# A conformer block on one core: the output product by Strassen's scheme in half the tokens first, norm weights moved to the transposed side

## The chip, the cores and the metric

The kernel runs on 1 core of one Trainium2 chip. The metric is the device time of one execution in microseconds (us). Five engines work beside each other, each through its own queue in program order: PE (matrix products and transposes), DVE and ACT (tiles of 128 partitions, in SBUF or in PE's accumulators, the PSUM banks), POOL (tiles in SBUF) and SP, which issues the DMAs. PE's clock is granted at one of two levels; the profile prints the granted share (1.00 or 0.50, and mixtures in a stretch).

## The reference

T = 1024 tokens, D = 1024, an inner width of 2816. Only the end of the block matters here:

```
g_att, g_conv = split(sigmoid(gate_logits))
mix = (g_att * y_att + g_conv * (conv @ w_conv_out)) @ w_o
x   = layer_norm(ALPHA * x + mix, ln1_g, ln1_b)
u   = x @ w_up ;  a, b = split(u)
ffn = (gelu(causal_dwconv(a, 3 taps)) * b) @ w_down
x   = layer_norm(ALPHA * x + ffn, ln2_g, ln2_b)
```

`layer_norm` is (x - mean) * rsqrt(var + eps) * g + b over the 1024 columns. Results are fp32.

## The kernel before

Every fp32 operand is split in two parts, a rounded high part (ACT copy) and a low part (DVE subtraction); a product is three matmuls, hi·hi, lo·hi and hi·lo. One matmul takes 128 rows of a weight or input and 512 columns. The stages, by the profiled execution: projections, attention, convolution and gates up to about 550 us; the product with w_conv_out up to 594; the output product with `w_o`; the first norm; up (22 steps called quads, each a two by two Strassen product of 84 matmuls) from about 700 to 1147; down (seven Strassen products of 11 steps, 12 matmuls each) up to 1367; the last norm and the output.

The work around the change:

- **Output product (L825 to L851).** `mix` (L655 to L672) is kept in two token halves. Half 0 runs k by k into eight banks, 192 matmuls; then tiles 4 to 7 run one at a time, 48 matmuls each: 384 in all. `close_tile` (L683) takes the banks into `res[t]` with the residual and row sums, and its `norm` squares on ACT (L696) and applies mean, scale, weight and bias in two 128x1024 DVE operations (L705, L706).
- **`turn0` (L748) and `turn1` (L761).** They transpose the normed tiles by PE (32 transposes each; `res` of tiles 0 to 3, then 4 to 7) and form the parts `xfh`/`xfl` of the seven left operands of the up Strassen products. `turn0`, called after tile 5, makes products 1 and 2's, `turn1` those of 4, 5, 7, 6, 3, in four rounds over k; POOL makes 8 sums (L773, L774).
- **Up.** `quad` (L884) runs products 1, 3, 2, 5, 7, 6, 4 of one weight block; `prep_raw` and `prep_sums` (L802 to L815) prepare the next block's parts and its four POOL sums `wt`. The x1 tiles go to DRAM after the turns.
- **Down.** `next_step` keeps the loads, POOL's sums `dn` of weights (L958, 44 of them) and the parts `hl..` (two ACT copies, two DVE subtractions of 128x512, L972 to L975) a step or more ahead. `step_load` reloads a tile of x1 with every second load of products 5 and 6. After product 6 come `p1` additions, POOL's `p5` subtractions (L1093) and 16 joins into `resb` (L1088), 12 of them in one run; the closing of tiles uses `close_tile` again and one output DMA of 512 KB a tile.

Each engine's queue order is set by the scheduler from program order and priorities; what stands where is shown below.

Of the kernel before, what the change touches and what calls it, by code (L numbers as in the profile page):

```python
# [115 lines left out]
def build(ctx, tc, xT, x, w_v, w_in, w_ao, w_co, w_o, w_up, w_dn, par, rel, rows, out):  # L116
# [538 lines left out]
    mix = [[], []]  # L655
    for s in range(8):
        if s % 2 == 0:
            w = next_w()
        wys = tuple(v[:, (s % 2) * HT:(s % 2 + 1) * HT] for v in w)
        o = bank2()  # L660
        for h in range(2):
            strip(o[:, h, :], wys, cv, KA, h)
        V.tensor_mul(t2[s], o.rearrange("p h t -> p (h t)"), t2[s])
        V.tensor_add(t2[s], t2[s], t1[s])
        for h in range(2):
            hi, lo = sb(f"mxh{h}{s}", [P, HT], F32R), sb(f"mxl{h}{s}", [P, HT], F32R)
            m = t2[s][:, h * HT:(h + 1) * HT]
            S.activation(hi, m, AF.Copy)
            V.tensor_sub(lo, m, f32(hi))
            mix[h].append((hi, lo))  # L670
        sb.free(t1[s], t2[s])
# [6 lines left out]
    def close_tile(t, scale, g_bc, b_bc, out=None):  # L678


        r, st = res[t], st_r()
# [8 lines left out]

        def norm():
            V.tensor_add(m, st[:, 0:1], st[:, 1:2])
            V.tensor_scalar(z, m, -1.0 / D, None, op0=OP.mult)
# [11 lines left out]
            V.scalar_tensor_tensor(r, r, m, g_bc, op0=OP.subtract, op1=OP.mult)  # L705
            V.scalar_tensor_tensor(r, r, y, b_bc, op0=OP.mult, op1=OP.add)  # L706
            if out is not None:
                nc.sync.dma_start(out, r)

        return take, norm  # L710

    def close_tiles(ts, banks, *a, outs=None):
        norms = []
        for t in ts:
            take, norm = close_tile(t, *a, out=None if outs is None else outs[t])
            for c, o in enumerate(banks(t)):
                take(o, c)
            norms.append(norm)
        for norm in norms:
            norm()  # L720

    def single(t, i):

        if t % 2 == 0 or i == 2:
            return bank()
        return ps_v.tile([P, HT], F32, tag="pv", name="pv") if i else ps_t.tile([P, HT], F32, tag="tp", name="tp")

    g_bc, b_bc = sb("g1", [P, D]), sb("b1", [P, D])
    bcast(g_bc, 0)
    bcast(b_bc, 1)  # L730
# [3 lines left out]

# [11 lines left out]

    def turn0():

        for n in (1, 2):
            part(n)  # L750
            xs[n] = [sb(f"xs{n}{i}", [P, HT]) for i in range(4)]
        for k in range(KD):
            n, i = 1 + k // 4, k % 4
            tp = bank()
            turned(tp, 0, k)
            hi, lo = xf[n][i]
            S.activation(hi, tp, AF.Copy)
            V.tensor_sub(lo, tp, f32(hi))
            S.activation(xs[n][i], tp, AF.Copy)
# [423 lines left out]
```

## Time and profile before

| | us |
|---|---|
| median of 3 runs | 1381.43 (1380.97 to 1382.74) |
| the profiled execution, its own time | 1380.95 |
| its span | 1379.2 |
| PE busy | 1334.7 (97%) |
| DVE busy | 977.7 (71%) |
| ACT busy | 605.6 (44%) |
| POOL busy | 350.6 (25%) |

The span is what the trace covers; 1.75 us of the execution lie around it. A busy share says how long an engine had an instruction in work; PE's waits must be looked for in the stretches where its share falls.

### The profile page before, as it was taken

Reading aid. Unit: us, or ns where it says so; the run is one execution under the profiler, and the core shown is the slowest. Engines: PE = TensorE matmul, PEld = TensorE weight load, DVE = VectorE, ACT = ScalarE, POOL = GpSimd, SP = SyncE. Lnnn points to the kernel's source line nnn. Section 1 sums busy time; section 2 is a strip of 40 time slices with the busy share of each in tenths; the row PEclk is TensorE's granted clock in tenths of the full one; section 3 lists DMA queues with packets and bytes.
Section 4 is the critical chain, followed back from the end, with each engine's and each line's share of the span. In section 5 each row is a group of like instructions: output and inputs, shape, how many; then the busy total and the mean of one; then the engine's idle time right before and its main releaser. Section 6 shows DMA issues by size and latency. Waiting matters only on the chain.

```text
span 1379.2 us, 16028 instructions
## 1 busy us (share of the span) xinstructions
PE 1334.7 (97%) x6004; PEld 1082.0 (78%) x6004; DVE 977.7 (71%) x1399; ACT 605.6 (44%) x916; POOL 350.6 (25%) x247
## 2 busy tenths in 40 slices
PE   9999999999999999999959999999999999998996
PEld 8877887887888888888737888888888878777885
DVE  5278888887799935746596565566666558997668
ACT  4346555656661137322453433334333444443453
POOL 1000000000000000000055566565555546972000
PEclk9999999999999999999969999999999999999999
DMA  7011111112101111621123323332223247753323
GB/s 268 16 46 41 40 56 41 56 51 82 47 31 46 55 37 52 223 92 51 45 62 107 108 87 115 115 115 89 103 96 103 100 173 267 263 166 93 92 84 123
DMA packets 48495, 132.29 MB, mean 96 GB/s; under 512 B 5393, under 2 KB 5529, under 8 KB 45601
## 3 DMA queue, kind: packets, MB, share of 16 engines
q1 hardware_dynamic: 48416, 131.26, 27.8%
q8 instruction: 47, 0.77, 0.2%
q14 instruction: 32, 0.25, 0.1%
HBM read 101.07 MB, written 30.17 MB: 95 GB/s over the span
## 4 chain that ended last, share of the span: by engine, by line
PE 82%; DVE 9%; ACT 3%; POOL 3%; issue 2%; DMA 1%; POOLq 0%; DVEq 0%; SPq 0%; ACTq 0%
PE mm L196 6%; PE mm L197 6%; PE mm L198 6%; PE s L196 5%; PE s L197 5%; PE s L198 5%; PE s L821 4%; PE s L822 4%; PE s L823 4%; PE mm L822 2%; PE mm L823 2%; PE mm L821 2%; PE s L1051 2%; PE s L1052 2%; PE tp L456 2%; PE s L1050 2%
## 5 line engine op out<-in xcount | busy, mean ns | idle before, releaser
L196 PE MATMUL mm<-xh,whi 128*128 128x512 f32 x384 | 157.9, 411 | 2.0 <-ACT qq L266 2.0
L414 DVE SCALAR_TENSOR_TENSOR acc<-hpad,par,acc 128x1024 f32<-128x1024 f32 x120 | 152.3, 1278 | 0.7
L198 PE MATMUL mm<-xh,wlo 128*128 128x512 f32 x384 | 151.8, 395 | 0.0
L197 PE MATMUL mm<-xl,whi 128*128 128x512 f32 x384 | 151.5, 395 | 0.0
L809 POOL TENSOR_TENSOR wt<-quad 128x512 f32<-128x512 f32 x22 | 28.3, 1288 | 467.7 <-ACT junk L696 375.9
L180 ACT ACTIVATE whi<-wraw 128x1024 fp32r<-128x1024 f32 x40 | 42.4, 1060 | 109.3 <-PE s L197 65.8
L798 DVE TENSOR_TENSOR wrl<-quad,wrh 128x1536 fp32r<-128x1536 f32 x22 | 42.7, 1942 | 60.8 <-ACT wrh L797 60.8
L198 PEld LDWEIGHTS mm<-xh,wlo 128*128 128x128 f32 x384 | 72.2, 188 | 15.1
L958 POOL TENSOR_TENSOR dn<-dn,dn 128x512 f32<-128x512 f32 x44 | 73.7, 1697 | 32.7 <-DMA actr<-act_d 14.7
L196 PEld LDWEIGHTS mm<-xh,whi 128*128 128x128 f32 x384 | 72.4, 189 | 11.9 <-ACT qq L266 2.9
L197 PEld LDWEIGHTS mm<-xl,whi 128*128 128x128 f32 x384 | 72.7, 189 | 9.2
L821 PE MATMUL s<-xfh,w24h 128*128 128x512 f32 x176 | 73.5, 418 | 2.1 <-DVE uU L912 1.9
L822 PE MATMUL s<-xfh,w24l 128*128 128x512 f32 x176 | 68.8, 391 | 0.0
L823 PE MATMUL s<-xfl,w24h 128*128 128x512 f32 x176 | 68.8, 391 | 0.0
L458 ACT ACTIVATE pth<-tp 128x512 fp32r<-128x512 f32 (+3 forms) x96 | 41.5, 433 | 54.1 <-PE tp L456 53.5
L181 DVE TENSOR_TENSOR wlo<-wraw,whi 128x1024 fp32r<-128x1024 f32 x40 | 48.7, 1219 | 23.0 <-ACT whi L180 22.8
L459 DVE TENSOR_TENSOR ptl<-tp,pth 128x512 fp32r<-128x512 f32 (+3 forms) x96 | 46.8, 488 | 18.5 <-ACT pth L458 17.9
L1014 DVE SCALAR_TENSOR_TENSOR y<-a,par,y 128x1024 f32<-128x1024 f32 x22 | 38.6, 1756 | 29.3 <-ACT y L1013 29.3
L439 ACT ACTIVATE p<-p,st 128x640 f32<-128x640 f32 (+2 forms) x64 | 44.4, 694 | 28.6 <-DVE st L437 28.0
L821 PE MATMUL mm<-xfh,wrh 128*128 128x512 f32 x132 | 52.8, 400 | 3.1 <-ACT xfh L777 3.1
L1013 ACT ACTIVATE y<-a,par 128x1024 f32<-128x1024 f32 x22 | 27.4, 1245 | 62.4 <-POOL a L914 57.5
L812 POOL TENSOR_TENSOR wt<-wt,quad 128x512 f32<-128x512 f32 x22 | 54.1, 2458 | 0.9
(567 smaller groups left out, 3842.2 us busy)
## 6 DMA issues: line engine op xcount, KB each, us to landing
quad<-in_w_up SPq DMA_DIRECT2D x22, 1024.0 KB, 5.2
actr<-act_d SPq DMA_DIRECT2D x77, 256.0 KB, 2.7
wraw<-in_w_in SPq DMA_DIRECT2D x32, 512.0 KB, 3.5
act_d<-u SPq DMA_DIRECT2D x44, 256.0 KB, 2.0
dn<-in_w_dn SPq DMA_DIRECT2D x44, 256.0 KB, 4.0
act_d<-y SPq DMA_DIRECT2D x33, 256.0 KB, 2.3
res<-in_x SPq DMA_DIRECT2D x8, 512.0 KB, 5.8
wraw<-in_w_o SPq DMA_DIRECT2D x8, 512.0 KB, 3.5
```

Source lines behind the costliest of these rows:

```text
L181: V.tensor_sub(lo, raws[i], f32(hi))
L196: PE.matmul(o, ah, bh, start=first, stop=False)
L197: PE.matmul(o, ah, bl, start=False, stop=False)
L198: PE.matmul(o, al, bh, start=False, stop=last)
L414: V.scalar_tensor_tensor(a, hp[:, j:j + T], col(C_CW + c * TAPS + j), a, op0=OP.mult, op1=OP.add)
L439: S.activation(pt, pt, AF.Exp, bias=st[:, 0:1], scale=-1.0, accum_out=st[:, 1:2])
L459: last_lo[0] = V.tensor_sub(pl[:, :w], o[:, :w], f32(ph)[:, :w])
L812: G.tensor_add(t[:, 3], t[:, 2], b[:, 3])
L821: PE.matmul(o, wh, xh, start=go, stop=False, skip_group_check=not first)
L822: PE.matmul(o, wl, xh, start=False, stop=False, skip_group_check=not first)
L823: PE.matmul(o, wh, xl, start=False, stop=i == 3, skip_group_check=not first)
L958: G.tensor_add(dn[j][d], dn[j][d], dn[j][b])
```

## The change

- **Output product by Strassen's two by two scheme** over token halves and column halves: seven products of 48 matmuls (4 token tiles, 4 k blocks, 3 parts) in the order 1, 5, 6, 3, 2, 7, 4. `w_o` comes in four quadrants of 1 MB; POOL makes 16 sums of 128x512 for the weights (`wo_add`) and 16 more for the left forms (`m5`, `m7`); ACT and DVE make 14 pairs of 128x1024 parts of weights (`wo_parts`) and 28 pairs of 128x512 parts of left forms (16 pairs before). The rows of w_conv_out are relaid so that strips come in the order 0, 4, 1, 5, ...
- **Token half 0 is complete after product 2**, the fifth; its tiles are closed then. Statistics come from `bn_stats`/`bn_aggr` on DVE instead of the square on ACT; `plain` writes (x - mean) * rstd with one ACT operation, and the first norm's weight and bias are applied per partition where `turned` evicts the transposes.
- `turn0` comes before product 4, which completes half 1. **Products 1 and 2 of quads 0 and 1** (48 matmuls) run before `turn1`; `quad_first` and `begun` finish these two quads. `turn1` makes forms 4 and 7 in its rounds, then 5, 6 and 3 by 12 POOL sums in a chain.
- **x1 is stored without weight and bias.** Each of its 8 reloads is followed by one DVE `scalar_tensor_tensor` (times ALPHA and g1) and one POOL addition (b1), both 128x1024. The 16 joins of down become additions; 12 of them stand after `down(7)` in the program. Final tiles are closed in halves with two output DMAs of 256 KB each.

```diff
@@ output product
+    for i in range(4):
+        w = next_w()
+        for s, c in ((i, 0), (i + 4, 1)):
...
+        mix_form(1, i, a11)
+        G.tensor_sub(m5, a21, a22)
+        mix_form(5, i, m5)
+        G.tensor_sub(m5, m5, a11)
+        mix_form(6, i, m5)
+        G.tensor_add(m5, m5, a12)
+        mix_form(3, i, m5)
+        G.tensor_sub(m7[i], a11, a21)
...
+            V.scalar_tensor_tensor(rc, o, sign, rc, op0=OP.mult, op1=OP.add)
+            V.bn_stats(st[:, 6 * c:6 * c + 6], rc)
...
+        def plain():
+            m, y = norm()
+            V.scalar_tensor_tensor(z, m, -1.0, y, op0=OP.mult, op1=OP.mult)
+            S.activation(r, r, AF.Identity, bias=z, scale=y)
...
+    xb = banks_x()
+    wo_product(2, xb, 0)
+    wo_add(1, 3)
+    wo_parts(1, 0)
...
+    for t in range(4):
+        lns[t][0](0, xb[t])
+        lns[t][2]()
+    yb = banks_y()
+    wo_product(7, yb, 1)
...
+        S.activation(a, o, AF.Identity, bias=col(C_B1 + k), scale=col(C_G1 + k))
...
+    turn0()
     for t in range(4):
+        for i in range(4):
+            wo_mm(4, yb, 0, t, i, True)
+        lns[t + 4][0](0, yb[t])
+        lns[t + 4][2]()
...
+    for o, w, u in ((oa[0], wr, "1"), (oa[1], wr1, "1b")):
+        product(o, w, 0, 1, True)
+        S.activation(tmp[u], o, AF.Copy)
+        product(o, w, 2, 2, False)
     turn1()
@@ down
                 nc.sync.dma_start(res[t], x1_d[t])
+                V.scalar_tensor_tensor(res[t], res[t], ALPHA, g1_bc, op0=OP.mult, op1=OP.mult)
+                G.tensor_add(res[t], res[t], b1_bc)
...
+        V.tensor_add(r, r, o)
```

PE, where the transposes of half 0 stand. Before, they follow the last matmuls of tile 5 (`woh`, `mxh` are parts of w_o and of the mix), and 12 matmuls of tile 6 come after the first eight:

```order
L196 MATMUL pv_4876<-woh47_4662,mxh17_4458 128x512
L197 MATMUL pv_4876<-wol47_4663,mxh17_4458 128x512
L198 MATMUL pv_4876<-woh47_4662,mxl17_4459 128x512
L745 MATMUL mm_4940<-ident_68,res0_4466 128x128 [waits DMAHW1_49,DVE_49]
L745 MATMUL mm_4940<-ident_68,res1_4467 128x128 [waits DMAHW3_49,DVE_49]
L745 MATMUL mm_4940<-ident_68,res2_4468 128x128 [waits DMAHW5_49]
L745 MATMUL mm_4940<-ident_68,res3_4469 128x128 [waits DMAHW6_49]
L745 MATMUL mm_4948<-ident_68,res0_4466 128x128
L745 MATMUL mm_4948<-ident_68,res1_4467 128x128
L745 MATMUL mm_4948<-ident_68,res2_4468 128x128
```

After, they follow the last matmuls of product 7 (`wop1`, `mfh7`), and the first of product 4 (`mfh4`) come behind:

```order
L732 MATMUL s2_4945<-wop1l_4495,mfh73_4804 128x512
L733 MATMUL s2_4945<-wop1h_4494,mfl73_4805 128x512
L845 MATMUL mm_5020<-ident_68,res0_4496 128x128 [waits DMAHW5_49,Activation_49]
L845 MATMUL mm_5020<-ident_68,res1_4497 128x128 [waits DMAHW1_49,Activation_49]
L845 MATMUL mm_5020<-ident_68,res2_4498 128x128 [waits DMAHW2_49,Activation_49]
L845 MATMUL mm_5020<-ident_68,res3_4499 128x128 [waits DMAHW3_49,Activation_49]
L845 MATMUL mm_5031<-ident_68,res0_4496 128x128
L845 MATMUL mm_5031<-ident_68,res1_4497 128x128
L845 MATMUL mm_5031<-ident_68,res2_4498 128x128
L845 MATMUL mm_5031<-ident_68,res3_4499 128x128
L731 MATMUL s2_4944<-wop0h_4173,mfh40_4876 128x512 [waits DVE_49]
```

The transposes stand behind all of products 1, 5, 6, 3, 2 and 7, and in front of all of product 4; all four tiles are needed for the first eight.

PE at the end of `turn1`'s forms. Before, the form of product 7 (`xfh7`) follows that of 3 (`xfh3`), the one that needs the longest chain of sums, and product 2 (`xfh2`, parts made long ago) stands between:

```order
L821 MATMUL s2_5421<-xfh70_5177,w13h_5149 128x512 [waits DVE_49,PE_49]
L822 MATMUL s2_5421<-xfh70_5177,w13l_5150 128x512
L823 MATMUL s2_5421<-xfl70_5178,w13h_5149 128x512
L821 MATMUL s2_5421<-xfh71_5179,w13h_5149 128x512
L822 MATMUL s2_5421<-xfh71_5179,w13l_5150 128x512
L823 MATMUL s2_5421<-xfl71_5180,w13h_5149 128x512
L821 MATMUL s2_5421<-xfh72_5181,w13h_5149 128x512 [waits Activation_49]
L821 MATMUL mm_5420<-xfh32_5197,wrh_4846 128x512 [waits Activation_49]
L822 MATMUL mm_5420<-xfh32_5197,wrl_4847 128x512
L822 MATMUL s2_5421<-xfh72_5181,w13l_5150 128x512
L823 MATMUL s2_5421<-xfl72_5182,w13h_5149 128x512 [waits DVE_49]
L823 MATMUL mm_5420<-xfl32_5198,wrh_4846 128x512 [waits DVE_49]
```

After, product 3 of quad 1 (`wr1`, into bank `pv`) stands ahead of product 7 of quad 0:

```order
L921 MATMUL mm_5522<-xfl53_5393,w13h_5211 128x512 [waits DVE_49]
L919 MATMUL pv_5608<-xfh30_5417,wr1h_5206 128x512 [waits Activation_49]
L920 MATMUL pv_5608<-xfh30_5417,wr1l_5207 128x512
L921 MATMUL pv_5608<-xfl30_5418,wr1h_5206 128x512 [waits DVE_49]
L919 MATMUL pv_5608<-xfh31_5421,wr1h_5206 128x512 [waits Activation_49]
L920 MATMUL pv_5608<-xfh31_5421,wr1l_5207 128x512
L921 MATMUL pv_5608<-xfl31_5422,wr1h_5206 128x512 [waits DVE_49]
L919 MATMUL pv_5608<-xfh32_5425,wr1h_5206 128x512 [waits Activation_49]
L920 MATMUL pv_5608<-xfh32_5425,wr1l_5207 128x512
L919 MATMUL s2_5523<-xfh70_5296,w13h_5211 128x512 [waits Activation_49]
L920 MATMUL s2_5523<-xfh70_5296,w13l_5212 128x512
```

Products 7, 6 and 3 of quad 0, 36 matmuls, now stand behind a matmul that needs the form `xfh32`, the third of the last four that are made.

POOL at the end of up and the start of down (`dn` weight sums of down, `u22`, `u5` to `u8` the last sums of up). Before:

```order
L914 TENSOR_TENSOR a1_5323<-a1_5323,ue_5333 128x512 [waits DVE_49]
L958 TENSOR_TENSOR dn1_0_7878<-dn1_0_7878,dn0_0_8164 128x512 [waits DMAHW6_49,DMAHW7_49,Activation_49,Pool_49]
L914 TENSOR_TENSOR u22_5336<-u12_5335,ue_5333 128x512 [waits DVE_49]
L958 TENSOR_TENSOR dn1_3_7887<-dn1_3_7887,dn0_3_8224 128x512 [waits DMAHW4_49,DMAHW2_49,DVE_49]
L958 TENSOR_TENSOR dn1_4_7890<-dn1_4_7890,dn0_4_8244 128x512 [waits DMAHW3_49,DVE_49]
L1029 TENSOR_TENSOR u5_5337<-y0_5326,y1_5327 128x512 [waits DMAHW0_49,DVE_49]
L1031 TENSOR_TENSOR u7_5339<-y0_5326 128x512 [waits DMAHW1_49]
L1030 TENSOR_TENSOR u6_5338<-u5_5337,y0_5326 128x512 [waits Pool_49]
```

After, with the b1 additions on the reloaded tiles `resb`:

```order
L1064 TENSOR_TENSOR dn1_0_7933<-dn1_0_7933,dn0_0_8224 128x512 [waits DMAHW5_49,DMAHW0_49,DVE_49]
L1064 TENSOR_TENSOR dn1_1_7936<-dn1_1_7936,dn0_1_8246 128x512 [waits DMAHW7_49,DMAHW1_49,DVE_49]
L1064 TENSOR_TENSOR dn1_3_7942<-dn1_3_7942,dn0_3_8288 128x512 [waits DMAHW3_49,DVE_49,Activation_49]
L1055 TENSOR_TENSOR resb0_8073<-resb0_8073,b1_8082 128x1024 [waits DMAHW2_49,DVE_49,DMAHW5_49,Activation_49,Pool_49]
L1055 TENSOR_TENSOR resb2_8075<-resb2_8075,b1_8082 128x1024 [waits DMAHW6_49,DVE_49,PE_49]
L1055 TENSOR_TENSOR resb3_8076<-resb3_8076,b1_8082 128x1024 [waits DMAHW5_49,DVE_49,PE_49]
L1018 TENSOR_TENSOR u22_5444<-u12_5443,ue_5441 128x512 [waits DVE_49]
L1064 TENSOR_TENSOR dn1_2_7939<-dn1_2_7939,dn0_2_8265 128x512 [waits DVE_49]
L1144 TENSOR_TENSOR u5_5688<-y0_5437,y1_5438 128x512 [waits DMAHW4_49,DVE_49]
```

Three 128x1024 additions stand ahead of the last quad's `u22`, and five more among the sums of down's weights.

## Rows read from the trace of the kernel before

**Rows 1.** The page: busy time, and the chain that ended last by engine.
```profile
PE 1334.7 (97%) x6004; PEld 1082.0 (78%) x6004; DVE 977.7 (71%) x1399; ACT 605.6 (44%) x916; POOL 350.6 (25%) x247
...
PE 82%; DVE 9%; ACT 3%; POOL 3%; issue 2%; DMA 1%; POOLq 0%; DVEq 0%; SPq 0%; ACTq 0%
```

**Rows 2.** Stretch, length, busy PE, PEld, DVE, ACT, POOL, granted clock, DMA.
```profile
550.00:594.00 44.00, 44.00 (x196) 36.44 (x195) 33.13 (x35) 16.53 (x22) 0.00 (x0) 1.00 0.59 203
594.00:690.00 96.00, 95.22 (x436) 77.78 (x434) 51.05 (x132) 28.95 (x48) 1.52 (x2) 1.00 0.15 59
690.00:700.00 10.00, 2.40 (x10) 2.01 (x11) 9.07 (x12) 4.12 (x6) 6.02 (x4) 0.67 0.41 115
700.00:710.00 10.00, 6.90 (x21) 4.42 (x21) 10.00 (x12) 6.99 (x13) 5.20 (x5) 0.50 0.16 67
710.00:720.00 10.00, 9.03 (x25) 5.88 (x24) 10.00 (x13) 4.99 (x9) 5.42 (x4) 0.64 0.01 2
720.00:760.00 40.00, 35.56 (x146) 26.78 (x146) 26.82 (x26) 15.95 (x17) 20.48 (x15) 1.00 0.32 105
```

**Rows 3.** Waits of PE, 594 to 770 us: total, times, longest.
```profile
PE s L745 <- DVE res L706: 7.4, 1, 7.4
PE mm L821 <- ACT xfh L777: 3.1, 3, 1.1
```

**Rows 4.** Stretches around the idle time of PE, as in group 2.
```profile
690.00:694.00 4.00, 0.00 (x0) 0.00 (x0) 3.90 (x7) 1.06 (x1) 3.92 (x3) 0.91 0.15 60
694.00:700.00 6.00, 2.40 (x10) 2.01 (x11) 5.17 (x6) 3.07 (x5) 2.10 (x2) 0.50 0.58 152
712.00:718.00 6.00, 6.00 (x15) 4.14 (x16) 6.00 (x8) 3.01 (x5) 2.82 (x3) 0.57 0.01 4
```

**Rows 5.** PE's instructions from 693 us: start, us, operation, idle before.
```profile
696.59 2.40 PE L745 MATMUL s<-ident,res 128*128 128x128 f32 x10 [7.35 <-DVE res L706]
...
721.10 0.50 PE L821 MATMUL mm<-xfh,wrh 128*128 128x512 f32 x1 [0.99 <-ACT xfh L777]
```

**Rows 6.** Groups by line, 680 to 760 us: count, busy, mean ns.
```profile
L778 DVE TENSOR_TENSOR xfl<-xs,xfh 128x512 fp32r<-128x512 f32 x20 | 19.6, 1041 | 0.0
...
L773 POOL TENSOR_TENSOR xs<-xs,xs 128x512 f32<-128x512 f32 x4 | 5.1, 1280 | 11.1 <-DVE xs L771 8.0 <-ACT u L895 3.1
...
L696 ACT ACTIVATE junk<-res,st 128x1024 f32<-128x1024 f32 x2 | 2.3, 1152 | 13.7 <-DVE st L693 13.7
```

**Rows 7.** Busy time by stretch, the down stage.
```profile
1120.00:1150.00 30.00, 28.80 (x126) 23.14 (x125) 19.80 (x26) 14.42 (x21) 6.08 (x4) 1.00 0.74 264
1150.00:1200.00 50.00, 48.52 (x211) 38.91 (x210) 49.00 (x37) 22.65 (x40) 43.99 (x27) 1.00 0.67 243
1200.00:1250.00 50.00, 47.71 (x204) 37.53 (x203) 48.81 (x43) 20.98 (x37) 39.38 (x25) 1.00 0.52 162
1250.00:1300.00 50.00, 46.09 (x197) 37.72 (x196) 33.45 (x57) 19.14 (x34) 0.54 (x1) 0.97 0.34 100
1300.00:1350.00 50.00, 50.00 (x222) 41.42 (x221) 33.81 (x87) 27.16 (x49) 0.00 (x0) 1.00 0.30 95
```

**Rows 8.** Groups of POOL by line, 1150 to 1250 us.
```profile
L958 POOL TENSOR_TENSOR dn<-dn,dn 128x512 f32<-128x512 f32 x43 | 72.4, 1707 | 18.0 <-DMA dn<-in_w_dn 9.2 <-DVE hl3wl L973 4.4 <-DVE hl4wl L973 1.3
```

**Rows 9.** DVE's instructions from 1236 us.
```profile
1238.22 0.68 DVE L975 TENSOR_TENSOR hl0al<-actr,hl0ah 128x512 fp32r<-128x512 f32 x1
1238.83 1.78 DVE L973 TENSOR_TENSOR hl0wl<-dn,hl0wh 128x512 fp32r<-128x512 f32 x1
...
1245.93 9.98 DVE L1088 SCALAR_TENSOR_TENSOR resb<-resb,p 128x512 f32<-128x512 f32 x11 [1.19 <-POOL p L1093]
```

**Rows 10.** Waits of PE, 1120 to 1379 us.
```profile
PE s L1051 <- DVE hl1wl L973: 4.3, 2, 3.9
```

**Rows 11.** The last instructions of the span: DVE and the output DMAs.
```profile
1372.16 3.68 SPq L708 DMA_DIRECT2D out<-resb  x2
...
1374.19 1.28 DVE L706 SCALAR_TENSOR_TENSOR resb<-resb,st,b 128x1024 f32<-128x1024 f32 x1
```

More of the change, by code (lines that the diff above doesn't have):

```diff
@@ L653, in build @@
         sb.free(*a)
[L655 to L671, printed above, removed]
+    h0, h1 = cols
@@ L672, in build, with wo_add @@
     for a in cv:
         sb.free(*a)
-    def bcast(dst, i):
-        nc.sync.dma_start(dst, bass.AP(tensor=rows.tensor, offset=rows.offset + i * D, ap=[[0, P], [1, D]]))
-    def close_tile(t, scale, g_bc, b_bc, out=None):
+    for r in (raw_r, whi_r, wlo_r):
+        r.close()
+    for i in (2, 3):
+        nc.sync.dma_start(wo[i], w_o[i])
+    wop.append(pair_of_parts("wop1", 4))
+    def wo_add(d, b):
+        for k in range(4):
+            G.tensor_add(wo[d][:, k], wo[d][:, k], wo[b][:, k])
@@ L704, in norm @@
             V.tensor_mul(y, y, z)
[L705 to L730, printed above, removed]
+            return m, y
+        def plain():
+            m, y = norm()
+            V.scalar_tensor_tensor(z, m, -1.0, y, op0=OP.mult, op1=OP.mult)
+            S.activation(r, r, AF.Identity, bias=z, scale=y)
+        return take, norm, plain
     res = [sb(f"res{t}", [P, D]) for t in range(8)]
@@ new lines, in build @@
+    for i in range(4):
+        mix_form(2, i, t2[i + 4][:, h0])
+    for t in range(4):
+        join(t, 0, p1[t])
+        V.tensor_add(p1[t], p1[t], xb[t])
+        G.tensor_sub(p5[t], p5[t], p1[t])
+        join(t, 1, p5[t])
+    yb = banks_y()
+    wo_product(3, yb, 1)
+    wo_parts(0, 3)
+    wo_add(0, 2)
+    for i in range(4):
+        mix_form(7, i, m7[i])
+    sb.free(*m7)
+    lns = [close_tile(t) for t in range(8)]
+    for t in range(4):
+        lns[t][0](1, yb[t])
+    xb = banks_x()
@@ L737, in build @@
+    wo_product(2, xb, 0)
+    wo_add(1, 3)
+    wo_parts(1, 0)
+    for i in range(4):
+        mix_form(4, i, t2[i + 4][:, h1])
+    sb.free(*t2)
+    for t in range(4):
+        join(t + 4, 1, p5[t])
+        join(t + 4, 0, p1[t])
+    sb.free(*p1, *p5)
+    for t in range(4):
+        lns[t][0](0, xb[t])
+        lns[t][2]()
+    yb = banks_y()
+    wo_product(7, yb, 1)
+    wo_parts(0, 1)
+    sb.free(*wo, *wop[1])
+    for t in range(4):
+        lns[t + 4][0](1, yb[t], -1.0)
     xf = {}
@@ L747, in turn0 @@
     def turn0():
         for n in (1, 2):
[L750 to L759, printed above, removed]
+            xs[n] = []
+            for i in range(4):
+                xs[n].append(turned(f"xs{n}{i}", bank(), 0, 4 * (n - 1) + i))
+                xf_form(n, i, xs[n][i])
@@ L780, in turn1 @@
+        for t in range(4, 8):
+            nc.sync.dma_start(x1_d[t], res[t])
+            sb.free(res[t])
+        for i in range(4):
+            xf_form(5, i, a21[i])
+            G.tensor_sub(a21[i], a21[i], xs[1][i])
+        for i in range(4):
+            xf_form(6, i, a21[i])
+            G.tensor_add(a21[i], a21[i], xs[2][i])
+        for i in range(4):
+            xf_form(3, i, a21[i])
+            sb.free(a21[i])
         sb.free(*xs[1], *xs[2])
@@ L1093, in build @@
         G.tensor_sub(p5[t], p5[t], p1[t])
+    y = banks_y()
+    down(7, y)
+    lns = [close_tile(t) for t in range(8)]
     for t in range(4):
@@ L1097, in build @@
         join(t, 1, p5[t])
-    y = banks_y()
-    down(7, y)
-    lns = [close_tile(t, 1.0, g_bc, b_bc, out[t]) for t in range(8)]
-    def take(t, c, o, sign=1.0):
-        lns[t][0](o, c, sign)
-    for t in range(4):
-        take(t + 4, 1, y[t], -1.0)
+        lns[t + 4][0](1, y[t], -1.0)
     x = banks_x()
```

296 lines of the change are left out of this document (178 added, 118 removed).

## The prediction

> **What bounds the kernel now.** I read the page first: PE is busy for 97% of the span and 82% of the chain that ended last is PE [rows 1]. So time is won in two ways only: fewer matmuls, or less time in which PE stands still. The reader is to see in the busy time by stretch where that is. At full pace 222 matmuls pass in 50 us in the last of [rows 7], 0.225 us each. Between 594 and 760 the output product, the first norm and the start of up run. There the rows count 436 + 10 + 21 + 25 + 146 = 638 PE instructions [rows 2]: 384 matmuls of the output product, 64 transposes, some 190 matmuls of up. Ten transposes take 2.40 us at half clock [rows 5], so one about 0.12 at full clock, and the work is 574 x 0.225 + 64 x 0.12 = 137 us. The stretch is 166 us long; **about 29 us are lost in it**, nearly all after 690.
>
> The waits of PE say on what: 7.4 us once on the norm of the last tile and 3.1 us on the forms that `turn1` makes [rows 3]. The stretches around the first wait show the second part of the loss: PE does nothing from 690 to 694, the granted clock is 0.50 in 694 to 700, still 0.57 in 712 to 718, and 1.00 from 720 on [rows 2, 4]. Those are the two levels, 1.2 and 2.4 GHz. In 712 to 718 PE was busy all the time and passed 15 instructions where 26.6 fit, so one such recovery costs 11.6 x 0.225 = 2.6 us.
>
> The down stage is the other place. From 1150 to 1250 DVE is busy for 97.8 us of 100, POOL for 83.4, and PE passes 415 instead of 444 matmuls: 6.5 us lost. From 1250 to 1300 it passes 197 of 222: 5.6 us, with 3.9 us in one wait [rows 7, 10]. That wait is behind a run of 11 joins on DVE, 9.98 us [rows 9].
>
> **The change, part by part.**
>
> *Fewer matmuls.* 48 x 0.225 = **10.8 us** of PE work go. Nothing else in the change takes matmuls away.
>
> *Strassen products 1 to 7.* ACT and DVE make 14 pairs of weight parts of 128x1024 and 28 of left forms, POOL 32 sums. DVE: 14 x 1.2 + 28 x 0.6 + 16 joins, 4 sums and 8 takes x 0.6 + 8 `bn_stats` x 0.6, about 55 us; an operation of 1024 columns is 1.28 long [rows 11], with a little less between two starts, one of 512 columns 0.68 [rows 9]. `bn_stats` has no row; between 0 and the 0.68 of a 512 column pass I take 0.6, since it reads 512 columns once. From 550 to 594 DVE is busy for 33 us [rows 2]; 16 subtractions of mix parts, 9.6 us, are in the 55 already, so 23 stay. POOL's sums slow DVE: a subtraction takes 1.78 where POOL works and 0.68 where it doesn't [rows 9], 1.1 us more for each sum it meets; 20 that meet one give 22. Together 100 us of DVE in the 117 from 550 to 667. For PE that is enough: two sets of weight parts take turns, and the chain for one, four POOL sums of 1.28 to 1.71 [rows 6, 8] and two pairs, 3.5, is 8.6 to 10.3 us long, against 10.8 for a product. I take **no wait** (bounds 0 and 10 us). The six products in front of the transposes end at 594 + 6 x 48 x 0.225 = 659.
>
> *The wait that remains.* PE's queue has the transposes of tiles 0 to 3 directly behind product 7, ahead of all of product 4. They need all four tiles normed. Product 2 ends at 648. DVE has for each tile a take and `bn_stats`, 0.6 each, and a chain of eight small operations, an estimated 0.8, to do: 2 us a tile, 8 us; before them some 3.5 us of joins and weight parts are queued, and the four sums of the first up block on POOL hold DVE for 4 x 1.1 us. 648 + 3.5 + 8 + 4.4 = 664, then the last scale on ACT, 1.15 for an operation of this shape [rows 6], and a few hand-overs: 667. So **PE waits 8 us** (bounds 2 and 13: without contention, or with one more set of weight parts in front), where before it waited 7.4; the clock falls again, and the recovery costs 2.6 us. Then come 32 transposes and 96 matmuls, 25.4 us, with about 1.5 us of small waits: PE is through at 667 + 25.4 + 2.6 + 1.5 = 696.5. The norm of tiles 4 to 7 is hidden behind the 48 matmuls of up: product 4 ends near 684, and the last tile needs some 10 us.
>
> *`turn1`.* Before, it took from 696.59, its first transposes, to 721.1, when the last wait for a form ends: 24.5 us [rows 5]. DVE is the pace there: 20 subtractions at 1.04 [rows 6]. The new one has the same 20 pairs, four other DVE subtractions fewer, and 12 chained POOL sums instead of 8, 1.28 to 1.7 each [rows 6, 8], so 15 to 20 us, which start with the first round. I keep 25 us: from about 694.5 to 720. In it PE has 32 transposes, products 4 and 5 of quad 0 and the start of product 3 of quad 1, 4 + 24 x 0.225 + 1.5 = 11 us. Since that product 3 stands ahead of 36 matmuls that would be ready, **12 to 14 us of PE stay empty.** At 720 some 80 matmuls of up are done; the 110 more, up to the 190 that before had done by 760, take 24.8 us and 2 of small waits: 747. **This part is 13 us faster** (5 to 20): 10.8 from the matmuls and 2 from smaller losses, 27 instead of 29.
>
> *Down.* The reload of x1 costs 8 DVE operations of 128x1024, 1.2 us each, and 8 POOL additions of that size, which no row has: by 1.28 for 512 columns [rows 6], between 2.2 and 2.6, I take 2.4. In this stretch the two engines slow each other. DVE's subtraction lasts 1.78 beside POOL and 0.68 without [rows 9], POOL's sums 1.71 against 1.28 [rows 6, 8]: POOL holds DVE for 1.1 of its 1.28 us. So the additions take 8 x 2.4 x 1.1 / 1.28 = 16 us from DVE, 26 with its own 9.6, where it has 2.2 us left of 100 [rows 7]. Three additions stand in POOL's queue ahead of the last quad's `u22`, and so of the activations that wait for it; the others stand between weight sums, behind which the steps' subtractions and then PE wait. The cover: from 1120 to 1150 DVE has 10 us free and POOL 24 [rows 7]; that takes 10 to 13, and parts are made a step or more ahead. Of the 13 to 16 left I expect 10 us on PE. Against that, the 12 joins now stand in DVE's queue among the parts of the next steps, two or three at a time; that returns the 5.6 us. **Net 4 us slower** (14 slower, the cover half gone, to 4 faster, nearly all hidden).
>
> The Trainium skill, page "SBUF — State Buffer", section "SBUF: two separate sides", says that DVE and GpSimd share one port pair as an exclusive lock, which an operation keeps for the whole instruction while the other is fully blocked. The trace bears the direction out, but 1.1 of 1.28 us is less than the whole; by the page the eight additions would take 19 us from DVE instead of 16, and the sum would come out 3 us higher.
>
> *Tail.* The last DVE operation is at 1374.19 and takes 1.28, output DMA 3.68 [rows 11]. `bn_stats` adds 1 us of DVE a tile net of the small operations it replaces; the way over ACT, 1.15 [rows 6], goes; four half operations instead of two whole cost 0.1; the last DMA is half as large. DVE was the pace of the last four tiles, so I take **1 us slower** (3 slower to 2 faster).
>
> **Sum**: 13 - 4 - 1 = 8 us. The profiled execution took 1380.95, its span 1379.2; the median of the runs is 0.5 above it, which the sum leaves aside: 1380.95 - 8 = **1373 us**.
>
> **Rivals.**
>
> *The port in down becomes the bound.* All 26 us fall on PE, less the 5.6 of the joins: 20 slower in down, 13 - 20 - 1 = -8, **1389 us**. It decides from where POOL ends the sums of a step later than PE ends the step before, 12 x 0.225 = 2.7 us each. For it: DVE at 49.00 and 48.81 of 50 [rows 7]. Against it: POOL has 6 and 10 us of 50 free there, and the last five additions stand singly in its queue. This is the case that ends on the slower side. Chance 0.13.
>
> *The seam closes.* The norm of half 0 is ready by 659 because contention is less, the clock stays at 1.00, and products of half 0 cover `turn1`: the loss between 594 and 760 is 14 instead of 27, 26 - 4 - 1 = 21, **1360 us**. Against it: the queue order of PE, and product 3 ahead of 7 and 6. Chance 0.17.
>
> *The Strassen stage starves.* The chain of POOL sums and weight parts is slower than a product, and PE stops for 2 us before each of five, 10 in all: 3 - 4 - 1 = -2, **1383 us**. For it: 10.3 of 10.8 us at the upper price, and DVE at 100 of 117. Against it: at the start nothing else is on POOL, and the quadrants can be loaded before 594, where DMA is busy 0.59 of the time [rows 2]. Chance 0.14.
>
> **How the numbers follow.** Forecast 0.56, within 1366 to 1379. A measurement of this kernel tells about 0.2% from no change, so faster means under 1378.7, slower over 1384.2. Faster: 0.17, most of the forecast's 0.56 and a little of the starving case, 0.73. Same: the rest of the forecast and most of the starving case, 0.12. Slower: 0.13 and the rest, 0.15. The range of 8 in 10 leaves out the half of the closing seam below 1360 and most of the port rival: **1360 to 1385**.
>
> **What would show it.** Right: 336 matmuls between 594 and about 684; one wait of PE of 5 to 10 us on ACT's scale of tile 3 near 659, with the granted clock at 0.50 behind it; a second, longer series of waits in 697 to 720 on forms 5, 6 or 3; up ending some 13 us earlier; PE in the hundred microseconds of products 1, 5, 6 below 415 instructions; no 3.9 us wait behind the joins. Wrong: waits inside the Strassen products, a seam without idle time, or down at the old pace with the additions in it. The number falls first with the down term, whose bounds lie farthest apart.

## The result, and the profile after

The changed kernel takes 1398.71 us (median of 4 runs, 1397.68 to 1399.51); the kernel before took 1382.09 (4 runs, 1380.97 to 1383.48). The ratio is 1.0119, with an interval of 1.0102 to 1.0137: **16.6 us slower**, where 8 us faster was predicted. The profiled spans are 1397.4 and 1379.2, 18.2 us apart. The kernel has 48 PE instructions fewer and waits longer for them; the first part of the page says who is busier [rows 1]:

```profile
PE 1331.2 (95%) x5956; PEld 1078.4 (77%) x5956; DVE 1040.7 (74%) x1401; ACT 617.4 (44%) x923; POOL 443.1 (32%) x295
```

DVE is busy 63 us longer than before, POOL 92 us. Where PE lost time, in three places:

**The output product to the start of up.** Busy time by stretch (length, then PE, PEld, DVE, ACT, POOL, granted clock, DMA share, GB/s), to be held against [rows 2]:

```profile
594.00:690.00 96.00, 88.06 (x381) 71.82 (x380) 84.01 (x132) 48.23 (x69) 43.52 (x26) 0.95 0.23 83
690.00:700.00 10.00, 9.99 (x46) 7.84 (x45) 5.23 (x24) 7.34 (x10) 0.24 (x1) 1.00 0.76 277
700.00:710.00 10.00, 7.43 (x39) 5.14 (x37) 6.02 (x8) 6.89 (x12) 3.84 (x3) 1.00 0.10 40
710.00:720.00 10.00, 6.17 (x19) 3.98 (x19) 9.96 (x9) 5.69 (x11) 7.65 (x7) 0.79 0.01 2
720.00:730.00 10.00, 4.19 (x7) 2.12 (x8) 10.00 (x9) 4.66 (x8) 8.34 (x5) 0.50 0.00 0
730.00:760.00 30.00, 27.66 (x114) 21.81 (x113) 23.32 (x23) 12.47 (x13) 13.85 (x9) 0.95 0.20 70
```

From 594 to 690 PE stood for 8 us where before it stood for 1. From 700 to 730 it passed 65 instructions, at a granted clock that fell to 0.50. Counted in the traces, 191 matmuls of up were begun by 760, 186 before: the stretch gained 5 x 0.225, 1 us, not 13. The waits of PE there (total, times, longest), against [rows 3]:

```profile
PE mm L731 <- ACT q L785: 4.3, 1, 4.3
PE mm L845 <- ACT res L770: 3.3, 2, 2.2
PE pv L919 <- ACT xfh L661: 3.3, 1, 3.3
PE mm L921 <- DVE xfl L662: 3.0, 2, 2.4
```

**Products 1, 5 and 6 of down**, against [rows 7], and the waits of PE in it, against [rows 10]:

```profile
1120.00:1150.00 30.00, 26.77 (x116) 21.26 (x115) 25.25 (x25) 13.86 (x19) 13.95 (x7) 1.00 0.72 241
1150.00:1200.00 50.00, 43.31 (x177) 34.72 (x175) 47.41 (x35) 20.98 (x37) 40.15 (x22) 0.93 0.60 205
1200.00:1250.00 50.00, 40.19 (x149) 30.16 (x150) 50.00 (x34) 15.89 (x28) 45.07 (x26) 0.90 0.51 162
1250.00:1300.00 50.00, 50.00 (x222) 41.40 (x222) 48.98 (x66) 20.79 (x36) 15.88 (x10) 1.00 0.41 123
```

```profile
PE s L1163 <- DVE hl4wl L1079: 4.4, 1, 4.4
PE mm L1164 <- DVE hl2al L1081: 3.6, 1, 3.6
PE s L1163 <- DVE hl0wl L1079: 3.1, 1, 3.1
```

From 1120 to 1250 PE passed 442 matmuls, before 541: 99 x 0.225 = 22 us less work done. From 1250 to 1300 it passed 222, before 197: 5.6 us came back. Net 16.7 us are lost, counted from an up stage that had been 1 us ahead.

**The tail.** The last matmul and DVE's last operations (start, us, operation), against [rows 11]:

```profile
1381.93 0.39 PE L1164 MATMUL pv<-hl4wh,hl4al 128*128 128x512 f32 x1
...
1393.02 1.42 DVE L1224 SCALAR_TENSOR_TENSOR resb<-resb,st,b 128x512 f32<-128x512 f32 x2
```

From the last matmul to the end of the span 15.5 us pass; before it was 12.4, from 1366.8 to 1379.2. The three places add up to 1 - 16.7 - 3.1 = -18.8 us, against -18.2 between the spans; the half microsecond left is less than three matmuls, which is about what counting at the edges of stretches can tell.

### The profile page after: what moved, and what is told of

Its sections match the earlier page's. It is cut to its first block, busy times and chain, and to the rows that moved or that the text cites. A ratio compares the mean times of both kernels' runs of the same rounds, so it can differ in the third digit from the quotient of the medians.

```text
span 1397.4 us, 16028 instructions
## 1 busy us (share of the span) xinstructions
PE 1331.2 (95%) x5956; PEld 1078.4 (77%) x5956; DVE 1040.7 (74%) x1401; ACT 617.4 (44%) x923; POOL 443.1 (32%) x295
## 4 chain that ended last, share of the span: by engine, by line
PE 74%; DVE 15%; ACT 4%; POOL 4%; issue 2%; DMA 1%; SPq 0%; DVEq 0%; POOLq 0%; ACTq 0%
PE mm L193 5%; PE mm L194 5%; PE mm L195 5%; PE s L919 4%; PE s L193 4%; PE s L194 4%; PE s L195 4%; PE s L921 4%; PE s L920 4%; PE mm L921 2%; PE mm L919 2%; PE mm L920 2%; PE s L1163 2%; PE s L1164 2%; PE s L1162 2%
## 5 line engine op out<-in xcount | busy, mean ns | idle before, releaser
L726 POOL TENSOR_TENSOR wo<-wo,wo 128x512 f32<-128x512 f32 x16 | 31.0, 1962 | 247.3 <-DVE wop0l L662 243.8
```

## The experiments

The kernel before, measured again beside these runs, took 1381.8 to 1382.4 us, so times of different runs can be compared to about half a microsecond. "Less" means less than the changed kernel's 1398.71 us where nothing else is said.

Two theories stood for the down stage. **A**: POOL's additions and sums, and DVE's work beside them, slow each other down, so that the parts of the steps come late. **B**: the weight and bias of the first norm are loaded late (g1 and b1 were issued at 1135; ACT then stood for 7.4 us in front of its scaling of b1, with parts behind it in its queue).

### Taking the additions and the multiplications away

Without the additions, without all of it, and without ACT's scaling only:

```diff
 d_noadd
-                G.tensor_add(res[t], res[t], b1_bc)
 d_plain
-                V.scalar_tensor_tensor(res[t], res[t], ALPHA, g1_bc, op0=OP.mult, op1=OP.mult)
-                G.tensor_add(res[t], res[t], b1_bc)
...
-    bcast(g1_bc, 0)
-    bcast(b1_bc, 1)
-    S.activation(b1_bc, b1_bc, AF.Copy, scale=ALPHA)
 d_noscale
-    S.activation(b1_bc, b1_bc, AF.Copy, scale=ALPHA)
```

> The changed kernel without the eight POOL additions of b1 to the reloaded x1 tiles; the loads of g1 and b1, ACT's scaling of b1 and the eight DVE multiplications stay. The residual lacks b1. Theory A (POOL and DVE slow each other in down): the additions, 2.84 us each in the trace of after, 22.7 us, and what they take from DVE go, so at least 12 of the 15 us that products 1, 5 and 6 lost come back: about 1385 us, and PE passes over 380 matmuls between 1150 and 1250 instead of 326. Theory B (ACT waits 7.4 us for the load of b1 in front of the scaling, and what stands behind it in its queue comes late): the wait stays, so at most 5 us come back: 1394 or more.

Measured: 1387.07 us, 11.6 less than the changed kernel. Busy time of d_noadd by stretch:

```profile
1150.00:1200.00 50.00, 45.31 (x190) 36.16 (x189) 45.39 (x37) 21.52 (x39) 39.73 (x23) 0.97 0.62 216
1200.00:1250.00 50.00, 45.04 (x193) 35.27 (x192) 49.45 (x44) 20.51 (x36) 37.59 (x24) 1.00 0.62 198
```

PE passes 383 matmuls instead of 326. A's number for the matmuls is met, its 12 us nearly; B's ceiling of 5 us is broken.

> The changed kernel without any weight or bias on the reloaded x1 tiles: no loads of g1 and b1, no scaling, no eight DVE multiplications, no eight POOL additions. The residual lacks ALPHA, g1 and b1. Theories A and B: down returns to the pace of before and keeps the joins' gain, 15 + 5 = 18 to 21 us less than the changed kernel: 1378 to 1381 us. If neither is the cause (another order of loads or joins costs the time): above 1388.

Measured: 1378.97 us, 19.7 less. Busy time by stretch:

```profile
1150.00:1200.00 50.00, 45.72 (x191) 36.95 (x190) 46.76 (x35) 21.32 (x38) 45.24 (x28) 0.93 0.65 228
1200.00:1250.00 50.00, 49.16 (x214) 39.71 (x213) 48.49 (x45) 22.82 (x40) 39.86 (x23) 1.00 0.59 182
```

PE passes 405 matmuls, near the 415 of before. Both theories allow that; it shows that nearly the whole loss in down, 19.7 of the 22 us, belongs to the weight and bias of the reloaded tiles: about 12 us to POOL's eight operations and 8 to DVE's eight with their loads.

> The changed kernel without ACT's scaling of b1 by ALPHA (b1 is added unscaled); loads, DVE multiplications and POOL additions stay. Theory B (ACT's 7.4 us wait for the load of b1 makes the parts behind it late): 3 to 6 us less than the changed kernel, 1393 to 1396. Theory A alone: the wait was beside other waits, within 1.5 us of 1398.7.

Measured: 1398.56 us, no change. The waits of PE in down, without the scaling:

```profile
PE s L1162 <- DVE hl4wl L1079: 4.1, 1, 4.1
PE mm L1163 <- DVE hl2al L1081: 3.6, 1, 3.6
PE s L1162 <- DVE hl0wl L1079: 3.0, 1, 3.0
```

They are the same three as in the changed kernel. **B falls**: without the scaling ACT stands at the same place for 11.7 us, now for a matmul of up, so the 7.4 us lay beside another wait.

### Moving POOL's sums to DVE

```diff
 d_alldve
-                G.tensor_add(res[t], res[t], b1_bc)
+                V.tensor_add(res[t], res[t], b1_bc)
...
-            G.tensor_add(dn[j][d], dn[j][d], dn[j][b])
+            V.tensor_add(dn[j][d], dn[j][d], dn[j][b])
```

> The changed kernel with the eight additions of b1 and the 44 weight sums of down on DVE instead of POOL. By the rows a POOL sum of 512 columns holds DVE for 1.1 us, the sum on DVE itself takes 0.6. Theory A: DVE in 1150 to 1250 has 80 parts and joins x 0.6, 43 sums x 0.6 and 10 operations of 1.2, 86 us of 100, so PE loses little there: down regains 12 to 15 us, 1384 to 1387. Rival (DVE's own count of operations is the bound, or its in-order queue waits for the weight loads that POOL waited for): 1394 or more.

Measured: 1373.46 us, **25.3 us less** than the changed kernel. Busy time by stretch, then two groups of DVE from 1150 to 1250 (count, busy, mean ns, idle before):

```profile
1150.00:1200.00 50.00, 49.55 (x219) 40.70 (x218) 49.85 (x66) 24.46 (x44) 6.64 (x4) 1.00 0.88 299
1200.00:1250.00 50.00, 50.00 (x222) 41.42 (x221) 48.57 (x77) 22.98 (x41) 5.97 (x4) 1.00 0.43 132
```

```profile
L1064 DVE TENSOR_TENSOR dn<-dn,dn 128x512 f32<-128x512 f32 x41 | 26.7, 684 | 1.4 <-DMA dn<-in_w_dn 1.4
...
L1054 DVE SCALAR_TENSOR_TENSOR resb<-resb,g 128x1024 f32<-128x1024 f32 x6 | 7.3, 1215 | 0.0
```

PE passes 441 of 444 matmuls, more than in the kernel before, although DVE now does 52 more operations in the whole of down. In these 100 us it passes 143 operations in 98.4 us of busy time; the changed kernel's DVE passed 69 in 97.4, the one before 80 in 97.8 [rows 7]. So much of what counts as busy beside POOL was time in which DVE did not get on. A sum on DVE costs it 0.68 us; the same sum on POOL had cost DVE 1.1. The multiplication by g1 takes 1.2 us here. In the changed kernel, from 1120 to 1250, it took 2.15 and POOL's addition 2.85, against the 1.2 and 2.4 that the prediction took:

```profile
L1054 DVE SCALAR_TENSOR_TENSOR resb<-resb,g 128x1024 f32<-128x1024 f32 x8 | 17.1, 2152 | 1.6 <-DMA g<-in_rows 0.8 <-DMA resb<-x_d 0.8
```

```profile
L1055 POOL TENSOR_TENSOR resb<-resb,b 128x1024 f32<-128x1024 f32 x8 | 22.7, 2850 | 5.0 <-DVE resb L1054 5.0
```

The edit gained 10 to 13 us more than A's figure. A had counted DVE's load and left a loss of some microseconds standing; with POOL quiet there is next to none, and what the kernel before lost here goes too. **A holds.** No run separates its two sides, the time that POOL takes from DVE and the lateness of what waits in POOL's own queue.

The same on the kernel before, with and without the move of the sums:

```diff
 b_joins (on the kernel before)
-    for t in range(4):
-        join(t + 4, 0, p1[t])
-        join(t + 4, 1, p5[t])
-        join(t, 1, p5[t])
     y = banks_y()
     down(7, y)
+    for t in range(4):
+        join(t + 4, 0, p1[t])
+        join(t + 4, 1, p5[t])
+        join(t, 1, p5[t])
 b_alldve: that, and
-            G.tensor_add(dn[j][d], dn[j][d], dn[j][b])
+            V.tensor_add(dn[j][d], dn[j][d], dn[j][b])
```

> The kernel before, with one edit: the twelve joins that follow product 6 of down stand behind product 7 in the program, as in the changed kernel. If the run of 11 joins on DVE was what PE waited for: the wait of 3.9 us and the lower clock behind it go, 5 to 6 us, about 1376.5 us. Rival: DVE is loaded anyway there, the joins only push other parts back, within 2 us of 1382.

Measured: 1375.24 us beside 1381.84 for the kernel before, ratio 0.9952 (0.9937 to 0.9967): 6.6 us. The stretch behind the joins, 197 matmuls in [rows 7]:

```profile
1250.00:1300.00 50.00, 50.00 (x223) 41.39 (x222) 37.07 (x64) 20.77 (x36) 1.52 (x1) 1.00 0.37 110
```

> The kernel before with the twelve joins behind product 7 and the 44 weight sums of down on DVE instead of POOL. Theory A: the 6.5 us that PE loses between 1150 and 1250 go as well as the 6.6 us of the joins: 1369 to 1371 us. Rival (DVE with 43 more operations is the bound): 1376 or more.

Measured: 1366.86 us beside 1381.91, ratio 0.9891 (0.9876 to 0.9906): 15.0 us, 8.4 of them from the weight sums alone, two more than PE's count of matmuls had shown as lost. PE is full:

```profile
1150.00:1200.00 50.00, 50.00 (x222) 41.42 (x221) 44.54 (x66) 23.12 (x41) 6.63 (x4) 1.00 0.80 274
1200.00:1250.00 50.00, 50.00 (x223) 41.40 (x222) 47.26 (x73) 23.74 (x42) 5.95 (x4) 1.00 0.48 148
```

### The first part: forms on POOL

```diff
 t_dve (turn1)
-            G.tensor_sub(a21[i], a21[i], a22)
+            V.tensor_sub(a21[i], a21[i], a22)
...
-            G.tensor_sub(a21[i], a21[i], xs[1][i])
+            V.tensor_sub(a21[i], a21[i], xs[1][i])
...
-            G.tensor_add(a21[i], a21[i], xs[2][i])
+            V.tensor_add(a21[i], a21[i], xs[2][i])
 f_dve (output product): the three lines of m5
-        G.tensor_sub(m5, a21, a22)
+        V.tensor_sub(m5, a21, a22)
...
```

> The changed kernel with turn1's twelve sums on DVE instead of POOL. If DVE's subtractions are slow there because POOL works beside them (1.78 or 1.7 instead of 0.6 us): 36 DVE operations of 0.6 take 22 us, the last form is ready 7 to 10 us earlier than at 730, PE's waits between 705 and 730 shrink and the clock stays at 1.00 longer: 1389 to 1393 us. Rival (transposes, ACT's hand-overs and the order of PE set the pace, DVE gets 12 operations more): 1397 to 1401.

Measured: 1390.24 us, 8.5 less. DVE's 20 subtractions of `turn1`, in the changed kernel and in this one (count, busy, mean ns), and this one's stretches:

```profile
L662 DVE TENSOR_TENSOR xfl<-xs,xfh 128x512 fp32r<-128x512 f32 x20 | 22.1, 1164 | 4.6 <-ACT xfh L661 4.6
```

```profile
L662 DVE TENSOR_TENSOR xfl<-xs,xfh 128x512 fp32r<-128x512 f32 x20 | 13.0, 686 | 3.8 <-ACT xfh L661 3.8
```

```profile
710.00:720.00 10.00, 8.37 (x33) 5.69 (x32) 10.00 (x18) 7.53 (x13) 0.00 (x0) 1.00 0.01 2
720.00:730.00 10.00, 9.38 (x38) 6.58 (x38) 10.00 (x15) 4.91 (x8) 3.29 (x2) 1.00 0.00 0
```

They take 0.69 instead of 1.16 us, twelve more operations stand among them, and yet the last form is there at 724.8 instead of 730.5, 5.7 us earlier (7 to 10 were expected). PE passes 71 instructions from 710 to 730 instead of 26, at full clock.

> The changed kernel with the twelve sums of the chain m5 (forms of products 5, 6 and 3) on DVE instead of POOL. If the 4.3 us wait of PE at 619 is ACT standing in order behind a form that POOL makes late, with the evictions of product 1 behind it: the wait goes, and the lower clock behind it, 4 to 7 us: 1392 to 1395. Rival (POOL's weight sums alone make the parts late, or the gain is lost in the wait before the transposes): within 2 us of 1398.7.

First, what the wait at 619 was. These are the changed kernel's ACT queue (in order) and POOL's: start, us, operation, and in brackets the idle time before it:

```profile
616.42 0.58 ACT L785 ACTIVATE q<-mm 128x512 f32<-128x512 f32 x1
621.03 0.63 ACT L661 ACTIVATE mfh<-m 128x512 fp32r<-128x512 f32 x1 [4.03 <-POOL m L708]
621.57 0.58 ACT L785 ACTIVATE q<-tp 128x512 f32<-128x512 f32 x1
```

```profile
615.97 3.36 POOL L726 TENSOR_TENSOR wo<-wo,wo 128x512 f32<-128x512 f32 x2 [1.16 <-DVE wop0l L662]
619.30 1.70 POOL L708 TENSOR_TENSOR m<-m,t 128x512 f32<-128x512 f32 x1
```

ACT evicted one bank of product 1 at 616.4, then stood for 4 us in front of a form of product 3 (L708), which POOL made behind two weight sums; the other three banks came after it, and product 6 waited for them. Measured: 1391.82 us, 6.9 less. The wait of 4.3 us is 0.8, and the one in front of the transposes, 3.3 in the changed kernel, grew to 4.2 only:

```profile
PE mm L845 <- ACT res L770: 4.2, 3, 2.2
...
PE mm L731 <- ACT q L785: 0.8, 1, 0.8
```

### The tail, and the edits together

```diff
 a_tail: as d_alldve, and the last eight tiles are closed as in the kernel before
-    lns = [close_tile(t) for t in range(8)]
+    def close_old(t):
...
+            V.scalar_tensor_tensor(rc, o, 1.0 if sign is None else sign, rc, op0=OP.mult, op1=OP.add,
+                                   accum_out=st[:, c:c + 1])
...
+            S.activation(junk, r, AF.Square, bias=z, accum_out=v)
...
+            V.scalar_tensor_tensor(r, r, m, g_bc, op0=OP.subtract, op1=OP.mult)
+            V.scalar_tensor_tensor(r, r, y, b_bc, op0=OP.mult, op1=OP.add)
+            nc.sync.dma_start(out[t], r)
...
+    lns = [close_old(t) for t in range(8)]
...
-        for c in cols:
-            V.scalar_tensor_tensor(r[:, c], r[:, c], m[0], g_bc[:, c], op0=OP.subtract, op1=OP.mult)
-            V.scalar_tensor_tensor(r[:, c], r[:, c], m[1], b_bc[:, c], op0=OP.mult, op1=OP.add)
-            nc.sync.dma_start(out[t][:, c], r[:, c])
+        lns[t][1]()
 a_best: the edits of d_alldve, t_dve and f_dve
 a_all: a_best, and
-        G.tensor_sub(m7[i], a11, a21)
+        V.tensor_sub(m7[i], a11, a21)
-            G.tensor_add(wo[d][:, k], wo[d][:, k], wo[b][:, k])
+            V.tensor_add(wo[d][:, k], wo[d][:, k], wo[b][:, k])
-        G.tensor_sub(p5[t], p5[t], p1[t])
+        V.tensor_sub(p5[t], p5[t], p1[t])
 b_best: b_alldve, and
-            G.tensor_sub(x6, x5, xs[1][i])
-            G.tensor_add(x3, x6, xs[2][i])
+            V.tensor_sub(x6, x5, xs[1][i])
+            V.tensor_add(x3, x6, xs[2][i])
```

> As the run with all down sums on DVE (1373.5 us), and the last eight tiles are closed as in the kernel before: row sums with the takes, the square on ACT, two DVE operations of 1024 columns, one output DMA of 512 KB. From the last matmul to the end of the span the changed kernel and all its variants take 15.5 us, the kernel before and its variants 12.4. If bn_stats and the halves on DVE are that difference: 12.4 again, 1370 to 1371. If it comes from the order of work in front of the last matmul: 1373 or more.

Measured: 1370.39 us, 3.1 less than d_alldve. The last matmul and DVE's last operation:

```profile
1355.77 0.39 PE L1164 MATMUL pv<-hl4wh,hl4al 128*128 128x512 f32 x1
...
1363.15 1.28 DVE L1234 SCALAR_TENSOR_TENSOR resb<-resb,st,b 128x1024 f32<-128x1024 f32 x1
```

From the last matmul to the end of the span at 1368.4 it is 12.6 us. The statistics and the closing in halves were put back together; what each costs alone was not run.

> The changed kernel with four edits together: additions of b1, weight sums of down, turn1's twelve sums and the m5 chain, all on DVE. Alone they gave 25.3 (the first two), 8.5 and 6.9 us. If they act in different places: 1398.7 - 25.3 - 8.5 - 6.9 = 1358 us. If the gains overlap (the wait before the transposes takes what the Strassen stage gives back): 1361 to 1366.

Measured: 1357.85 us beside 1382.4 for the kernel before, ratio 0.9822 (0.9808 to 0.9837), to the microsecond the sum of the parts. By stretch, and the longest wait that is left in the first part:

```profile
594.00:690.00 96.00, 90.83 (x400) 74.02 (x399) 89.99 (x156) 52.27 (x75) 38.61 (x21) 0.96 0.27 95
690.00:760.00 70.00, 61.18 (x260) 46.08 (x260) 50.33 (x62) 35.10 (x48) 27.14 (x19) 0.98 0.22 82
1150.00:1250.00 100.00, 100.00 (x443) 82.83 (x442) 97.65 (x149) 46.36 (x82) 5.96 (x4) 1.00 0.60 197
```

```profile
PE s L919 <- DVE ue L1011: 4.6, 1, 4.6
```

> As the run before with, besides, the sixteen w_o sums, the four m7 forms and the four p5 subtractions of the output product on DVE: POOL does nothing between 550 and 660. If POOL's sums cost DVE more than DVE's own: 0 to 3 us less than a_best. Rival: DVE is full between 600 and 667, so 24 operations of 0.6 more make the norm of half 0 later: up to 5 us more than a_best.

Measured: 1357.29 us (1355.92 to 1360.46), not to be told from a_best: neither the gain nor the loss showed.

> The kernel before with the twelve joins behind product 7, the weight sums of down and turn1's eight sums on DVE. Against 1366.9 without the last: DVE's 20 subtractions in turn1 take 0.6 to 0.7 instead of 1.04 us each, 8 more of its own come, so the forms are ready 2 to 4 us earlier: 1363 to 1365. Rival (the 7.3 us wait on the norm and the clock set it): 1367.

Measured: 1364.82 us, 2.0 less than b_alldve. The last matmuls of a_best and of b_best (start, us, operation), in spans of 1355.5 and 1362.4 us:

```profile
1340.00 0.39 PE L1164 MATMUL pv<-hl4wh,hl4al 128*128 128x512 f32 x1
```

```profile
1350.07 0.39 PE L1052 MATMUL pv<-hl4wh,hl4al 128*128 128x512 f32 x1
```

So with many of POOL's sums moved on both sides, the change as a whole is worth 7 us (1357.85 against 1364.82). By 760 us a_best had begun 260 matmuls of up, b_best 201: 59 x 0.225 = 13.3 us ahead. At the last matmul 10.1 are left of them, at the end of the span 6.9. That is 13 - 3 - 3, beside the 13 - 4 - 1 of the prediction. The agreement is in part luck, because the prediction meant a kernel whose sums are on POOL. The tail, which a_best still has, costs 3 us; a_best with the tail of before was not run.

## Why the prediction was wrong

The sum had 13 - 4 - 1 us and the spans show 1 - 16.7 - 3.1. Two steps failed by some 12 us each: the first part, where late forms were taken to cost nothing in the Strassen products and 25 us in `turn1`, and down, where most of the new work was taken to be hidden. One cause runs through both, the sums on POOL; the experiments show it, since moving sums to DVE gave back 8.5 and 6.9 us in the first part and 25.3 in down. Of the signs that the prediction named for being wrong, one came: a wait inside the Strassen products.

*Fewer matmuls, 10.8 us*: right; 336 are there, and in a_best and b_best, where little else stands in the way, the change shows its gain.

*"I take no wait" in the Strassen products*: wrong, though inside its bounds of 0 and 10. The six products in front of the transposes ended at 667.8, not 659. 2.3 us were lost before them in w_conv_out's strips, 4.3 in one wait, and about 2 in the lower clock behind it. The sum for DVE (100 of 117 us) was not what failed. What was missing is who waits for whom in ACT's queue: a form that POOL makes late held up three evictions that had nothing to do with it. The rival of the starving stage had the place, but not the mechanism; f_dve showed it.

*The wait in front of the transposes, 8 us*: too long, 3.3 in two pieces, where before it was 7.4 [rows 3]; the products before it were late, so the norm was ready sooner after them. The clock fell all the same, as forecast.

*`turn1`, ready at 720 with 12 to 14 us of PE empty*: the place and the order on PE were right, the size was not. It began at 698 and its last form was there at 730.5. From 700 to 730 PE passed 39 matmuls and 26 transposes, 12 us of work at full clock, so 18 us were lost. The step that failed is "I keep 25 us": it took 32.5. With the sums on DVE (t_dve) the same forms take 27.4, from 697.5 to 724.8. So some 5 of the 7.5 us too many come from the twelve POOL sums, which were priced as POOL's own time, starting early, and not as what they do to DVE. Its last twelve subtractions took 1.3 us each:

```profile
714.72 15.90 DVE L662 TENSOR_TENSOR xfl<-xs,xfh 128x512 fp32r<-128x512 f32 x12
```

The rest lies near the start, also in t_dve: twelve matmuls of product 2 stand between the first six transposes and the next, and DVE stood for 2.3 us before the first of its forms of product 7. t_dve gave back 8.5 us; with f_dve it is 15.4, more than the 12 us by which this part missed.

*Down, 4 us slower*: 16.7, beyond its own worst bound of 14. The prediction's price for the new work on DVE was 26 us, 16 for what the additions take and 9.6 for the multiplications; taking the two away gave back 11.6 and 8.1. (A multiplication lasted 2.15 us instead of 1.2, but what it loses to POOL is in the 16 already.) So the mechanism was right, and the price was, if anything, high. The step that failed is the cover, "that takes 10 to 13", with "of the 13 to 16 left I expect 10 us on PE": 19.7 us fell on the kernel's time. The rival of the port, with 20 us net, was nearer than the forecast. From 1120 to 1150 DVE used some 5 of its 10 free us, and PE passed 116 instructions instead of 126. The loads of g1 and b1 and the multiplications came at 1141, when the last products of up needed the same engines, and the first three additions ran as one block in front of `u22`, the order that the prediction had named:

```profile
1143.90 8.54 POOL L1055 TENSOR_TENSOR resb<-resb,b 128x1024 f32<-128x1024 f32 x3 [5.01 <-DVE resb L1054]
1152.40 1.72 POOL L1018 TENSOR_TENSOR u<-u,ue 128x512 f32<-128x512 f32 x1
```

`u22` came out of POOL at 1154, and the tiles of the last quad and a part `hl2` came from DVE behind it, while the steps had begun; PE waited 3.6 us for that part. The joins' 5.6 us came back as forecast.

*What a POOL sum takes from DVE*: the price in the trace, 1.1 us of DVE for each POOL sum of 1.28, was used for new work only. The old work paid it too: moving the 44 weight sums off POOL made the kernel before 8.4 us faster (b_alldve against b_joins). The Trainium skill, page "GPSIMD Engine Reference", section "4.1 Engine selection", gives elementwise sums to VectorE (DVE here), because GPSIMD (POOL) takes about twice as long. The trace agrees, 0.68 against 1.28, and goes further: beside a busy DVE, a POOL sum costs DVE more than the sum itself would.

*Tail, 1 us slower*: 3.1, a term mis-sized. DVE's last operation ended 12.5 us after the last matmul instead of 8.7, 3.8 later, and the halved last DMA gave back 0.8. One us of DVE a tile over four tiles, which DVE paces, is 4, so that price fits; against it the prediction took off the way over ACT, 1.15, which in the kernel before lay beside DVE's work and cost nothing. That split is read from the rows; a_tail shows only the 3.1 us together. `bn_stats` itself was priced well, 0.68 in its row and 0.60 to the next start:

```profile
693.36 0.68 DVE L754 BATCH_NORM_STATS2 st<-res 128x6 f32<-128x512 f32 x1
```

## What to carry to other kernels

Where DVE is near its limit, count an operation on POOL by what it takes from DVE, not by POOL's idle share: here 1.1 us for each sum of 512 columns, which DVE does itself in 0.68. Moving 44 such sums and 8 additions of twice the size to the busier engine made the kernel 25 us faster. When a change adds work to a stretch, price every operation as it runs in that stretch, beside its neighbours, and follow each in-order queue that the added work stands in: three of ACT's evictions behind one late form made PE wait 4.3 us.

## What the hardware showed that was not expected

- DVE and POOL do not share evenly: a subtraction of two SBUF tiles went from 0.68 to 1.78 us beside POOL [rows 9], while the sums on POOL went from 1.28 to 1.71 [rows 6, 8]. Together they got less done than DVE alone: with 52 operations more on DVE it was busy for 48.6 to 49.9 us of 50, and PE passed 441 matmuls of 444, where it had passed 326.
- The granted clock fell after short waits too. In the row below PE had waited 2.2 and 1.1 us for the normed tiles; from 720 to 730, with seven matmuls, the clock was 0.50. Such stretches cost more than their idle time: behind the 4.3 us wait, from 623.9 to 626.9, matmuls started 0.43 us apart instead of 0.225.

```profile
670.00:680.00 10.00, 8.20 (x34) 6.92 (x35) 7.98 (x15) 8.17 (x12) 0.00 (x0) 0.66 0.91 324
```
